# A batched matrix product: one batch per load with transposes on TensorE, against four batches per load with 32x32 transposes on VectorE

## Chip, cores and metric

One core of a Trainium2 chip runs the kernel. The metric is the device time of one execution in microseconds (us), taken as the median over several runs of the same program. The five engines of a core are called PE (TensorE; PEld is its loading of weights), DVE (VectorE), ACT (ScalarE), POOL (GpSimd) and SP (SyncE, which here only issues transfers). Sixteen DMA engines move data between the device memory (HBM) and the on-chip memory SBUF, which has 128 partitions. PE writes its results to a second on-chip memory, PSUM[...].

## What is computed

```python
# x: (32, 256, 512) float32, y: (32, 512, 384) float32
def reference(x, y):
    return np.einsum('bij,bjk->bik', x, y).astype(np.float32)
```

For each of 32 batches a 256 x 512 matrix is multiplied by a 512 x 384 matrix. The inputs are 41.94 MB, the output is 12.58 MB. PE sums over partitions, so the summed index j has to lie on the partitions of both operands. y arrives that way; x has to be transposed.

## The kernel before

Work is done one batch at a time. `load(b)` (L54 to L60) issues two transfers on SP's queue. Partition p of the x tile gets rows 2p and 2p+1 of the batch, 4 KB in one run; partition q of the y tile gets rows 4q to 4q+3, 6 KB in one run. So the j that lies on partition q in step t is 4q + t, for both operands.

`transpose(b)` (L62 to L72) makes x^T on PE: for each t of four it transposes the columns `t::NJ` of both row sets r with an identity matrix, in float32, into one PSUM tile (L68), which DVE (L70, t even) or ACT (L72, t odd) copies to SBUF as float16. `round_y(b)` (L74 to L81) rounds y to float16 in four pieces of 384 elements per partition, two on ACT (L79) and two on DVE (L81). `multiply(b)` (L83 to L99) does eight matmuls (L92), four steps t for each of two row sets r, each of which sums over 128 partitions and streams 384 columns. `collect(b)` copies the two results from PSUM to SBUF, one on ACT (L107) and one on DVE (L109), and `store(b)` (L120) issues one transfer of 3 KB per partition on SP.

What sets the order is the loop at L122 to L137 with `keep`, which keeps the instructions of each engine in program order. Five batches are loaded ahead. In step s the program loads batch s+5, collects s-2, transposes and rounds s, multiplies s-1 and stores s-2. In the last full step the matmuls come ahead of the transposes. All loads and stores share SP's queue, in this order, so a store that waits for its results holds back the loads written behind it. Buffers: seven each for x and y, eight for the output, four PSUM banks for transposes and four for results.

Of the kernel before, what the change touches and what calls it, by code (L numbers as in the profile page):

```python
# [1 line left out]

# [5 lines left out]


MM_DT = mybir.dt.float16  # L10
F32 = mybir.dt.float32
P = 128
AHEAD = 5
GROUPS = [1, 1, 1, 1, 1, 1, 1, 1, 1, 1, 1, 1, 1, 1, 1, 1, 1, 1, 1, 1, 1, 1, 1, 1, 1, 1, 1, 1, 1, 1, 1, 1]

@with_exitstack
def kernel(
    ctx: ExitStack,  # L20
    tc: tile.TileContext,
    x: bass.AP,
    y: bass.AP,
    out: bass.AP,
):
    nc = tc.nc

    B, I, J = x.shape
    _, _, K = y.shape

    NI = I // P
    NJ = J // P

    const_pool = ctx.enter_context(tc.tile_pool(name="const", bufs=1))
    x_pool = ctx.enter_context(tc.tile_pool(name="x_pool", bufs=AHEAD + 2))
    y_pool = ctx.enter_context(tc.tile_pool(name="y_pool", bufs=AHEAD + 2))
    yr_pool = ctx.enter_context(tc.tile_pool(name="yr_pool", bufs=4))
    xt_pool = ctx.enter_context(tc.tile_pool(name="xt_pool", bufs=4))
    o_pool = ctx.enter_context(tc.tile_pool(name="o_pool", bufs=8))
    tpsum_pool = ctx.enter_context(tc.tile_pool(name="tpsum", bufs=4, space=bass.MemoryType.PSUM))  # L40
    opsum_pool = ctx.enter_context(tc.tile_pool(name="opsum", bufs=4, space=bass.MemoryType.PSUM))


    keep = tc.keep_in_program_order

    identity = const_pool.tile([P, P], F32)
    make_identity(nc, identity)


    place = [(g, i, n) for g, n in enumerate(GROUPS) for i in range(n)]  # L50
    assert len(place) == B
    x_of, y_of, yr_of, xt_of, ps_of, o_of = {}, {}, {}, {}, {}, {}

    def load(b):  # L54


        x_of[b] = x_pool.tile([P, NI, J], F32, name="x_sb")
        y_of[b] = y_pool.tile([P, NJ, K], F32, name="y_sb")
        keep(nc.sync.dma_start(out=x_of[b], in_=x[b].rearrange("(p r) j -> p r j", p=P)))  # L59
        keep(nc.sync.dma_start(out=y_of[b], in_=y[b].rearrange("(q t) k -> q t k", q=P)))  # L60

    def transpose(b):  # L62
        x_sb = x_of.pop(b)
        xt_of[b] = xt_pool.tile([P, NJ, NI, P], MM_DT, name="xt_sb")
        for t in range(NJ):
            t_ps = tpsum_pool.tile([P, NI, P], F32, name="t_ps")
            for r in range(NI):
                keep(nc.tensor.transpose(t_ps[:, r], x_sb[:, r, t::NJ], identity))  # L68
            if t % 2 == 0:
                keep(nc.vector.tensor_copy(xt_of[b][:, t], t_ps))  # L70
            else:
                keep(nc.scalar.copy(xt_of[b][:, t], t_ps))  # L72

    def round_y(b):  # L74
        y_sb = y_of.pop(b)
        yr_of[b] = yr_pool.tile([P, NJ, K], MM_DT, name="y_r")
        for t in range(NJ):
            if t % 2 == 0:
                keep(nc.scalar.copy(yr_of[b][:, t], y_sb[:, t]))  # L79
            else:  # L80
                keep(nc.vector.tensor_copy(yr_of[b][:, t], y_sb[:, t]))  # L81

    def multiply(b):  # L83
        xt_sb, y_r = xt_of.pop(b), yr_of.pop(b)
        ps_of[b] = [
            opsum_pool.tile([P, K], F32, name=f"o_ps_{r}", tag="o_ps")
            for r in range(NI)
        ]
        for t in range(NJ):
            for r in range(NI):  # L90
                keep(
                    nc.tensor.matmul(  # L92
                        ps_of[b][r],
                        xt_sb[:, t, r],
                        y_r[:, t],
                        start=(t == 0),
                        stop=(t == NJ - 1),
                    )
                )  # L99

    def collect(b):
        g, i, n = place[b]
        if i == 0:
            o_of[g] = o_pool.tile([P, n, NI, K], F32, name="o_sb", tag=f"o_sb_{min(n, 2)}")
        for r in range(NI):
            if r % 2 == 0:
                keep(nc.scalar.copy(o_of[g][:, i, r], ps_of[b][r]))  # L107
            else:
                keep(nc.vector.tensor_copy(o_of[g][:, i, r], ps_of[b][r]))  # L109
        del ps_of[b]  # L110

    def store(b):
        g, i, n = place[b]
        if i < n - 1:
            return
        o_sb = o_of.pop(g)
        dst = out[b - i : b + 1].rearrange("b (p r) k -> p b (r k)", p=P)
        src = o_sb.rearrange("p b r k -> p b (r k)")
        if n == 1:
            keep(nc.sync.dma_start(out=dst[:, 0], in_=src[:, 0]))  # L120

    for b in range(AHEAD):  # L122
        load(b)
    for s in range(B + 2):
        if s + AHEAD < B:
            load(s + AHEAD)
        if s >= 2:
            collect(s - 2)
        if s == B - 1:
            multiply(s - 1)  # L130
        if s < B:
            transpose(s)
            round_y(s)
        if 1 <= s != B - 1 and s <= B:
            multiply(s - 1)
        if s >= 2:
            store(s - 2)  # L137


# [1 line left out]
_INS = ['x', 'y']  # L141
_OUTS = [((32, 256, 384), 'float32')]


# [23 lines left out]
```

## Time and profile before

| what | value |
|---|---|
| median of 8 runs | 137.29 us (137.19 to 137.57) |
| the profiled execution's own time | 137.42 us |
| its span, first to last instruction | 135.6 us |
| mean granted PE clock | 0.984 of full speed |
| busy: PE, PEld, DVE, ACT | 84.0, 58.6, 64.2, 66.7 us |
| DMA: bytes, mean rate | 54.64 MB, 403 GB/s |
| L68 transposes on PE, 256 | 40.6 us busy |
| L92 matmuls, 256 | 48.7 us busy, 336 ns mean of one |
| L70 and L72, transposes from PSUM, 64 each | 26.9 and 23.8 us busy, 423 and 372 ns |
| L79 and L81, rounding y, 64 each | 29.6 and 20.1 us busy, 509 and 355 ns |
| L109 and L107, results from PSUM, 32 each | 17.8 and 15.1 us busy, 557 and 471 ns |

The page cuts the span into 40 equal slices of 3.39 us. In the rows of engines each digit is the busy share of a slice in tenths; the DMA row is the mean share of the 16 DMA engines, and the row GB/s is what they moved. A row of a group names the line, the engine, the operation, the tile written and the tile read, the shape, how often it ran, its busy time and the mean duration of one. Consecutive instructions of an engine can overlap, so the busy time can be less than the count times the mean. The chain of waits goes back from the last instruction to what released it, and so on to the start; its shares say what the time was spent on.

### The profile page before, as it was taken

Reading aid. Unit: us, or ns where it says so; the run is one execution under the profiler, and the core shown is the slowest. Engines: PE = TensorE matmul, PEld = TensorE weight load, DVE = VectorE, ACT = ScalarE, POOL = GpSimd, SP = SyncE. Lnnn points to the kernel's source line nnn. Section 1 sums busy time; section 2 is a strip of 40 time slices with the busy share of each in tenths; the row PEclk is TensorE's granted clock in tenths of the full one; section 3 lists DMA queues with packets and bytes.
Section 4 is the critical chain, followed back from the end, with each engine's and each line's share of the span. In section 5 each row is a group of like instructions: output and inputs, shape, how many; then the busy total and the mean of one; then the engine's idle time right before and its main releaser. Section 6 shows DMA issues by size and latency. Waiting matters only on the chain.

```text
span 135.6 us, 1739 instructions
## 1 busy us (share of the span) xinstructions
PE 84.0 (62%) x512; PEld 58.6 (43%) x512; DVE 64.2 (47%) x160; ACT 66.7 (49%) x161; POOL 0.7 (1%) x6
## 2 busy tenths in 40 slices
PE   0579878855956765556765556775556775559610
PEld 0466555535534554334554333554333554335500
DVE  0344765643455544446544446544546544545510
ACT  3246866642556544456544456544456644446610
POOL 2000000000000000000000000000000000000000
PEclk9999999997799999999999999999999999999998
DMA  4999999999999999999999999999999999999992
GB/s 137 413 420 423 414 416 414 417 410 417 414 419 413 427 418 419 420 419 423 418 421 413 419 421 421 428 410 419 422 422 421 414 423 418 419 422 418 411 414 94
DMA packets 13833, 54.64 MB, mean 403 GB/s; under 512 B 1536, under 2 KB 1536, under 8 KB 13824
## 3 DMA queue, kind: packets, MB, share of 16 engines
q1 hardware_dynamic: 13824, 54.53, 98.6%
q8 instruction: 4, 0.07, 0.2%
q14 instruction: 5, 0.04, 0.1%
HBM read 41.94 MB, written 12.58 MB: 402 GB/s over the span
## 4 chain that ended last, share of the span: by engine, by line
DMA 90%; SPq 2%; PE 1%; issue 1%; DVE 0%; ACT 0%; ACTq 0%
DMA y_sb<-in_y_dram 43%; DMA out_dram<-o_sb 24%; DMA x_sb<-in_x_dram 23%; SPq L59 1%; PE o_ps L92 1%; SPq L60 1%; DVE o_sb L109 0%; ACT y_r L79 0%; SPq L120 0%; ACTq L79 0%
## 5 line engine op out<-in xcount | busy, mean ns | idle before, releaser
L68 PE MATMUL t_ps<-identity,x_sb 128*128 128x128 f32 x256 | 40.6, 305 | 44.1 <-DMA x_sb<-in_x_dram 41.5
L68 PEld LDWEIGHTS t_ps<-identity,x_sb 128*128 128x128 f32 x256 | 35.0, 211 | 54.8 <-DVE o_sb L109 44.0
L72 ACT CAST xt_sb<-t_ps 128x256 f16<-128x256 f32 x64 | 23.8, 372 | 52.5 <-issue 40.0
L92 PE MATMUL o_ps<-y_r,xt_sb 128*128 128x384 f16 x256 | 48.7, 336 | 1.2 <-ACT y_r L79 1.2
L70 DVE CAST xt_sb<-t_ps 128x256 f16<-128x256 f32 x64 | 26.9, 423 | 45.9 <-PE t_ps L68 44.0
L79 ACT CAST y_r<-y_sb 128x384 f16<-128x384 f32 x64 | 29.6, 509 | 7.4 <-DMA y_sb<-in_y_dram 7.3
L92 PEld LDWEIGHTS <-xt_sb 128*128 128x128 f16 x256 | 26.1, 102 | 15.6 <-issue 3.1
L81 DVE CAST y_r<-y_sb 128x384 f16<-128x384 f32 x64 | 20.1, 355 | 13.2 <-DMA y_sb<-in_y_dram 13.2
L109 DVE COPY o_sb<-o_ps 128x384 f32<-128x384 f32 x32 | 17.8, 557 | 6.6 <-PE o_ps L92 5.1
L107 ACT COPY o_sb<-o_ps 128x384 f32<-128x384 f32 x32 | 15.1, 471 | 2.4 <-PE o_ps L92 2.4
L72 ACT ACT_TABLE_LOAD x1 | 1.3, 1283 | 0.7 <-PEq L152 0.7
masks.py:199 POOL TENSOR_SCALAR_AFFINE_SELECT identity<-identity 128x128 f32<-128x128 f32 x1 | 0.3, 292 | 0.1
masks.py:197 POOL MEMSET identity<- 128x128 f32 x1 | 0.2, 205 | 0.3 <-POOLq L152 0.3
L152 POOL MEMSET const-bfloat16-1.0<- 128x1 bf16 x1 | 0.1, 101 | 0.0
L152 POOL MEMSET const-uint8-127<- 128x1 uint8 x1 | 0.1, 101 | 0.0
L152 POOL MEMSET const-float32-0.0<- 128x1 f32 x1 | 0.1, 98 | 0.2 <-issue 0.2
L152 POOL MEMSET const-float32-1.0<- 128x1 f32 x1 | 0.1, 98 | 0.0
## 6 DMA issues: line engine op xcount, KB each, us to landing
y_sb<-in_y_dram SPq DMA_DIRECT2D x32, 768.0 KB, 11.2
x_sb<-in_x_dram SPq DMA_DIRECT2D x32, 512.0 KB, 10.2
out_dram<-o_sb SPq DMA_DIRECT2D x32, 384.0 KB, 10.9
```

The source lines that it names most:

```text
L59: keep(nc.sync.dma_start(out=x_of[b], in_=x[b].rearrange("(p r) j -> p r j", p=P)))
L60: keep(nc.sync.dma_start(out=y_of[b], in_=y[b].rearrange("(q t) k -> q t k", q=P)))
L68: keep(nc.tensor.transpose(t_ps[:, r], x_sb[:, r, t::NJ], identity))
L70: keep(nc.vector.tensor_copy(xt_of[b][:, t], t_ps))
L72: keep(nc.scalar.copy(xt_of[b][:, t], t_ps))
L79: keep(nc.scalar.copy(yr_of[b][:, t], y_sb[:, t]))
L81: keep(nc.vector.tensor_copy(yr_of[b][:, t], y_sb[:, t]))
L92: nc.tensor.matmul(ps_of[b][r], xt_sb[:, t, r], y_r[:, t], start=(t == 0), stop=(t == NJ - 1),)
L107: keep(nc.scalar.copy(o_of[g][:, i, r], ps_of[b][r]))
L109: keep(nc.vector.tensor_copy(o_of[g][:, i, r], ps_of[b][r]))
L152: nc = _bacc.Bacc("TRN2", target_bir_lowering=False, num_devices=1)
```

## The change

Four batches form a chunk, and there are eight chunks. Each batch of a chunk has 32 of the 128 partitions.

- `load_x(n)` is one transfer of 2 MB: partition p of a batch's 32 gets rows 8p to 8p+7, 16 KB in one run. `load_y(n)` is one transfer of 3 MB: partition q gets rows 16q to 16q+15, 24 KB in one run. The last chunk's y comes in two transfers, 12 KB runs.
- `transpose_x(n)` no longer uses PE. ACT rounds x to float16 and lays out pairs of rows so that two float16 values make one 32-bit word, in four copies of 1024 elements per partition, reading with a step of 16 elements (64 bytes). After each, DVE transposes 32 x 32 blocks of such words, 512 words per partition. No identity matrix is made any more.
- `round_y(n)` rounds the chunk's y in eight pieces of 768 elements, five on DVE and three on ACT, in the order of `ROUND`.
- `multiply(n)` sums over 32 partitions at a time: for each of 16 steps c and two row sets e, four matmuls, one for each batch g, on that batch's 32 partitions, each into a PSUM bank of its own. That is 128 matmuls of 384 columns in a chunk, 1024 in all. All eight banks hold the results of one chunk.
- `collect(n)` is as before, eight copies for a chunk. `store(b)` still moves one batch, 3 KB per partition.
- The order: after the loads of x chunks 0 and 1 and y chunk 0, step n loads x chunk n+2 and y chunk n+1, rounds and multiplies chunk n, transposes chunk n+1, collects chunk n, and issues the stores of chunk n-1. The last two chunks' stores come last. There are two buffers each for x, the transposed x, y and rounded y, one for the packed x, and twelve for the output.

The diff, cut to its core:

```diff
--- before.py
+++ after.py
@@ -3,16 +3,22 @@
 import concourse.bass as bass
 import concourse.tile as tile
 from concourse import bass_utils, mybir
-from concourse.masks import make_identity
 from concourse._compat import with_exitstack
 MM_DT = mybir.dt.float16
 F32 = mybir.dt.float32
 P = 128
-AHEAD = 5
-GROUPS = [1, 1, 1, 1, 1, 1, 1, 1, 1, 1, 1, 1, 1, 1, 1, 1, 1, 1, 1, 1, 1, 1, 1, 1, 1, 1, 1, 1, 1, 1, 1, 1]
+Q = 4
+LATE = 8
+LAST = 2
+ROUND = (1, 0, 1, 1, 0, 1, 0, 1)
 @with_exitstack
@@ -28,113 +34,129 @@
     B, I, J = x.shape
     _, _, K = y.shape
-    NI = I // P
-    NJ = J // P
-    const_pool = ctx.enter_context(tc.tile_pool(name="const", bufs=1))
-    x_pool = ctx.enter_context(tc.tile_pool(name="x_pool", bufs=AHEAD + 2))
-    y_pool = ctx.enter_context(tc.tile_pool(name="y_pool", bufs=AHEAD + 2))
-    yr_pool = ctx.enter_context(tc.tile_pool(name="yr_pool", bufs=4))
-    xt_pool = ctx.enter_context(tc.tile_pool(name="xt_pool", bufs=4))
-    o_pool = ctx.enter_context(tc.tile_pool(name="o_pool", bufs=8))
-    tpsum_pool = ctx.enter_context(tc.tile_pool(name="tpsum", bufs=4, space=bass.MemoryType.PSUM))
-    opsum_pool = ctx.enter_context(tc.tile_pool(name="opsum", bufs=4, space=bass.MemoryType.PSUM))
+    S = P // Q
+    R = I // S
+    C = J // S
+    NE = I // P
+    A = R // NE // 2
+    N = B // Q
+    x_pool = ctx.enter_context(tc.tile_pool(name="x_pool", bufs=2))
+    xr_pool = ctx.enter_context(tc.tile_pool(name="xr_pool", bufs=1))
+    xt_pool = ctx.enter_context(tc.tile_pool(name="xt_pool", bufs=2))
+    y_pool = ctx.enter_context(tc.tile_pool(name="y_pool", bufs=2))
+    yr_pool = ctx.enter_context(tc.tile_pool(name="yr_pool", bufs=2))
+    o_pool = ctx.enter_context(tc.tile_pool(name="o_pool", bufs=12))
+    psum_pool = ctx.enter_context(tc.tile_pool(name="psum", bufs=Q * NE, space=bass.MemoryType.PSUM))
     keep = tc.keep_in_program_order
-    identity = const_pool.tile([P, P], F32)
-    make_identity(nc, identity)
+    x_of, y_of, xt_of, o_of = {}, {}, {}, {}
+    def load_x(n):
+        x_of[n] = x_pool.tile([P, R, J], F32, name="x_sb")
+        keep(
+            nc.sync.dma_start(
+                out=x_of[n],
+                in_=x[n * Q : (n + 1) * Q].rearrange("g (p r) j -> (g p) r j", r=R),
+            )
+        )
+    def load_y(n):
+        y_of[n] = y_pool.tile([P, C, K], F32, name="y_sb")
+        src = y[n * Q : (n + 1) * Q].rearrange("g (p c) k -> (g p) c k", c=C)
+        w = C // (LAST if n == N - 1 else 1)
+        for c in range(0, C, w):
+            keep(nc.sync.dma_start(out=y_of[n][:, c : c + w], in_=src[:, c : c + w]))
+    def transpose_x(n):
-    place = [(g, i, n) for g, n in enumerate(GROUPS) for i in range(n)]
-    assert len(place) == B
-    x_of, y_of, yr_of, xt_of, ps_of, o_of = {}, {}, {}, {}, {}, {}
-    def load(b):
-        x_of[b] = x_pool.tile([P, NI, J], F32, name="x_sb")
-        y_of[b] = y_pool.tile([P, NJ, K], F32, name="y_sb")
-        keep(nc.sync.dma_start(out=x_of[b], in_=x[b].rearrange("(p r) j -> p r j", p=P)))
-        keep(nc.sync.dma_start(out=y_of[b], in_=y[b].rearrange("(q t) k -> q t k", q=P)))
-    def transpose(b):
-        x_sb = x_of.pop(b)
-        xt_of[b] = xt_pool.tile([P, NJ, NI, P], MM_DT, name="xt_sb")
-        for t in range(NJ):
-            t_ps = tpsum_pool.tile([P, NI, P], F32, name="t_ps")
-            for r in range(NI):
-                keep(nc.tensor.transpose(t_ps[:, r], x_sb[:, r, t::NJ], identity))
-            if t % 2 == 0:
-                keep(nc.vector.tensor_copy(xt_of[b][:, t], t_ps))
-            else:
-                keep(nc.scalar.copy(xt_of[b][:, t], t_ps))
-    def round_y(b):
-        y_sb = y_of.pop(b)
-        yr_of[b] = yr_pool.tile([P, NJ, K], MM_DT, name="y_r")
-        for t in range(NJ):
-            if t % 2 == 0:
-                keep(nc.scalar.copy(yr_of[b][:, t], y_sb[:, t]))
-            else:
-                keep(nc.vector.tensor_copy(yr_of[b][:, t], y_sb[:, t]))
-    def multiply(b):
-        xt_sb, y_r = xt_of.pop(b), yr_of.pop(b)
-        ps_of[b] = [
-            opsum_pool.tile([P, K], F32, name=f"o_ps_{r}", tag="o_ps")
-            for r in range(NI)
-        ]
-        for t in range(NJ):
-            for r in range(NI):
+        x_sb = x_of.pop(n)
+        xr = xr_pool.tile([P, A, NE, C, S], F32, name="x_r")
+        xt = xt_pool.tile([P, C, NE, S, A], F32, name="xt_sb")
+        for a in range(A):
+            for e in range(NE):
                 keep(
-                    nc.tensor.matmul(
-                        ps_of[b][r],
-                        xt_sb[:, t, r],
-                        y_r[:, t],
-                        start=(t == 0),
-                        stop=(t == NJ - 1),
+                    nc.scalar.copy(
+                        xr[:, a, e].bitcast(MM_DT).rearrange("q c (j w) -> q w c j", w=2),
+                        x_sb[:, a * 2 * NE + e : (a + 1) * 2 * NE : NE].rearrange(
+                            "q w (j c) -> q w c j", c=C
+                        ),
                     )
                 )
+                keep(nc.vector.transpose(xt[:, :, e, :, a], xr[:, a, e]))
+        xt_of[n] = xt
-    def collect(b):
-        g, i, n = place[b]
-        if i == 0:
-            o_of[g] = o_pool.tile([P, n, NI, K], F32, name="o_sb", tag=f"o_sb_{min(n, 2)}")
-        for r in range(NI):
-            if r % 2 == 0:
-                keep(nc.scalar.copy(o_of[g][:, i, r], ps_of[b][r]))
+    def round_y(n):
+        y_sb = y_of.pop(n)
+        y_r = yr_pool.tile([P, C, K], MM_DT, name="y_r")
+        w = C // len(ROUND)
+        for k, dve in enumerate(ROUND):
+            part = slice(k * w, (k + 1) * w)
+            if dve:
+                keep(nc.vector.tensor_copy(y_r[:, part], y_sb[:, part]))
             else:
-                keep(nc.vector.tensor_copy(o_of[g][:, i, r], ps_of[b][r]))
-        del ps_of[b]
+                keep(nc.scalar.copy(y_r[:, part], y_sb[:, part]))
+        return y_r
+    def multiply(n, y_r):
+        xt_sb = xt_of.pop(n)
+        ps = [[psum_pool.tile([P, K], F32, name="o_ps") for e in range(NE)] for g in range(Q)]
+        for c in range(C):
+            for e in range(NE):
+                for g in range(Q):
+                    rows = slice(g * S, (g + 1) * S)
+                    keep(
+                        nc.tensor.matmul(
+                            ps[g][e],
+                            xt_sb[rows, c, e].rearrange("q p a -> q (p a)").bitcast(MM_DT),
+                            y_r[rows, c],
+                            start=(c == 0),
+                            stop=(c == C - 1),
+                        )
+                    )
+        return ps
+    def collect(n, ps):
+        for g in range(Q):
+            o_sb = o_of[n * Q + g] = o_pool.tile([P, NE, K], F32, name="o_sb")
+            for e in range(NE):
+                if e % 2 == 0:
+                    keep(nc.scalar.copy(o_sb[:, e], ps[g][e]))
+                else:
+                    keep(nc.vector.tensor_copy(o_sb[:, e], ps[g][e]))
     def store(b):
-        g, i, n = place[b]
-        if i < n - 1:
-            return
-        o_sb = o_of.pop(g)
-        dst = out[b - i : b + 1].rearrange("b (p r) k -> p b (r k)", p=P)
-        src = o_sb.rearrange("p b r k -> p b (r k)")
-        if n == 1:
-            keep(nc.sync.dma_start(out=dst[:, 0], in_=src[:, 0]))
+        keep(nc.sync.dma_start(out=out[b].rearrange("(m e) k -> m e k", m=P), in_=o_of.pop(b)))
-    for b in range(AHEAD):
-        load(b)
-    for s in range(B + 2):
-        if s + AHEAD < B:
-            load(s + AHEAD)
-        if s >= 2:
-            collect(s - 2)
-        if s == B - 1:
-            multiply(s - 1)
-        if s < B:
-            transpose(s)
-            round_y(s)
-        if 1 <= s != B - 1 and s <= B:
-            multiply(s - 1)
-        if s >= 2:
-            store(s - 2)
+    load_x(0)
+    load_x(1)
+    load_y(0)
+    transpose_x(0)
+    for n in range(N + 1):
+        if n + 2 < N:
+            load_x(n + 2)
+        if n + 1 < N:
+            load_y(n + 1)
+        if n < N:
+            ps = multiply(n, round_y(n))
+        if n + 1 < N:
+            transpose_x(n + 1)
+        if n < N:
+            collect(n, ps)
+        for b in range(max((n + 1) * Q - LATE, 0), min((n + 2) * Q - LATE, B) if n < N else B):
+            store(b)
 # ---- launch: one core; inputs and outputs as the reference has them ----
```

## The prediction

> **What bounds the kernel now.** I read the slices of the page first, then the DMA queues, the chain of waits, and last the windows and the groups.
>
> ```profile
> DMA  4999999999999999999999999999999999999992
> GB/s 137 413 420 423 414 416 414 417 410 417 414 419 413 427 418 419 420 419 423 418 421 413 419 421 421 428 410 419 422 422 421 414 423 418 419 422 418 411 414 94
> DMA packets 13833, 54.64 MB, mean 403 GB/s; under 512 B 1536, under 2 KB 1536, under 8 KB 13824
> q1 hardware_dynamic: 13824, 54.53, 98.6%
> DMA 90%; SPq 2%; PE 1%; issue 1%; DVE 0%; ACT 0%; ACTq 0%
> ```
>
> The 16 DMA engines are full from the second slice to the last but one; the chain is 90% transfers. No compute engine is above 62% of the span. So the time is bytes over rate, plus a start and an end. 13824 packets are 96 transfers of 128 runs (12288) and 1536 small ones, 16 for each transfer, which I take to be its completion. A run is now one packet: 4 KB for x, 6 KB for y, 3 KB for the output. The windows give the rate in steady state, at the end where only stores are left, and the clock around a pause of PE (columns: window and length; busy us and instructions of PE, PEld, DVE, ACT, POOL; clock; DMA share; GB/s):
>
> ```profile
> 40.00:60.00 20.00, 12.51 (x80) 8.72 (x80) 10.17 (x25) 10.23 (x25) 0.00 (x0) 1.00 1.02 420
> 130.00:130.50 0.50, 0.00 (x0) 0.00 (x0) 0.00 (x0) 0.00 (x0) 0.00 (x0) 1.00 1.01 406
> 130.50:131.00 0.50, 0.00 (x0) 0.00 (x0) 0.00 (x0) 0.00 (x0) 0.00 (x0) 1.00 1.03 418
> 30.00:32.00 2.00, 0.00 (x0) 0.02 (x1) 0.90 (x3) 1.08 (x3) 0.00 (x0) 1.00 0.98 405
> 32.00:34.00 2.00, 1.99 (x9) 1.83 (x10) 0.86 (x3) 0.39 (x2) 0.00 (x0) 0.54 1.05 430
> 34.00:36.00 2.00, 2.00 (x8) 0.83 (x6) 0.52 (x2) 1.20 (x4) 0.00 (x0) 0.61 1.00 408
> ```
>
> PE paused for 2.92 us and then ran about 3.5 us at a little over half its clock; the usual pauses of 1.6 to 2 us did not bring that. The timeline shows what it does to the eight matmuls of a batch:
>
> ```profile
> 33.74 2.36 PE L92 MATMUL o_ps<-y_r,xt_sb 128*128 128x384 f16 x8
> 41.52 1.46 PE L92 MATMUL o_ps<-y_r,xt_sb 128*128 128x384 f16 x8
> ```
>
> At full clock the last of eight lasts 0.326, so seven steps take 1.46 - 0.326 = 1.13 us, 162 ns each, and the weight loads between them are hidden. At half clock a step is twice that, 0.32.
>
> [...]
>
> **Part 1, the loads.** 64 loads become 8 of x (2 MB, 16 KB runs) and 9 of y (3 MB, 24 KB runs, the last in two halves); 32 stores stay as they are. Transfers fall from 96 to 49, runs from 12288 to 6272. The bytes, 54.53 MB, stay. At 420 GB/s they take 129.8 us[...]. A second reading: stores alone run at about 416 in 129 to 132 us, which takes 0.945 us for 0.393 MB; a batch at 420 takes 4.057 us, leaving 3.112 for its two loads of 1.311 MB. Solving for a cost per byte and per transfer gives 429 GB/s and 29 ns, so 47 x 29 ns = 1.4 us. That rests on half-microsecond readings from 406 to 424, so I take **2.2 us gained**. [...] Below nothing would need long runs that move slower than 4 KB ones; the trace cannot exclude it, and I keep 1 us for it.
>
> **Part 2, transposes and casts.** 256 transposes on PE (L68) and 128 copies from PSUM (L70, L72) go. In come 32 ACT copies of 1024 elements with x rounded[...] and 32 DVE transposes of 512 words. The trace has no DVE transpose: [...]it is about 0.69; twice that at worst. Rounding y is 24 ACT pieces of 768 (0.83 us) and 40 DVE pieces (355 ns plus 384 more at L81's pace, about 0.55). Collecting stays, 32 each at 471 and 557. A round of four batches costs ACT 3 x 0.83 + 4 x 1.04 + 4 x 0.47 = 8.5 us, DVE 5 x 0.55 + 4 x 0.69 + 4 x 0.56 = 7.8. Before it was 66.7/8 = 8.3 and 64.2/8 = 8.0. A round of transfers is 6.8 MB, 16 us. This is nothing while it lies under the transfers.
>
> **Part 3, the matmuls.** 1024 matmuls on 32 rows replace 256 on 128. If four run together, a pack of four takes 162 ns and a round 32 x 0.162 = 5.2 us. But PE now pauses about 9 us between rounds, so by the window above it starts at half clock: 3.5 us for 11 packs, then 21 x 0.162 = 3.4, with the last one's latency D = 7.1 us. In the middle that is hidden under 16 us.
>
> **Part 4, the start.** x0, x1 and y0 (7.34 MB) land at 2.3 (first bytes, from 182 GB/s in the first 4 us) + 17.1 + 0.8 (the first transposes started 0.8 us after their bytes were in) = 20.2 us. SP holds load 3 of x until ACT has rounded y0 (2.5) and copied x1 (4.2): 26.9. It must issue by 31.6 - 1.5 = 30.1 (1.5 us lie between the first issue and the first bytes). Slack 3.2 us, so nothing; copies at double cost just use it up. The loads of y wait only for rounding, done earlier; stores are eight batches late and wait for nothing on SP until the end.
>
> **Part 5, the end.** After y6 the queue holds four batches' stores, y7, then three times four batches' stores: 6.29 MB at 416 and 3.15 at 429, 22.4 us to the last byte. The four last stores need this chain after y6's bytes: landing 0.8, first rounding 0.5, D of round 6, four DVE collects 2.2 and rounding 0.55 (in program order on DVE ahead of the next matmuls), D of round 7, the first collect 0.56, issue to bytes 1.5, the stores 3.8: 9.9 + D6 + D7. There is room for D6 + D7 = 12.5. D6 is 7.1. D7 follows a pause of about 2.9 us, just where the trace had the clock fall: 5.4 if warm, 7.1 if not. The loss is 0 to 1.7; I take **0.9 lost**. y7's second half lands later than y6's chain needs only by less than this.
>
> **Sum.** The profiled execution took 137.42 (span 135.6 and 1.82 around it). -2.2 + 0.9 = -1.3 gives 136.1; it lies 0.13 above the median of the runs shown, so the forecast is **136.0**.
>
> **Rivals.** *The end of PE's chain takes the place of the queue* (slower): weight loads of 98 ns at full clock and 152 at half differ by 54 ns[...]; four in turn make a pack 213 ns, 427 at half clock. D is then 3.5 + 24 x 0.213 = 8.6, and the loss 2 x 8.6 - 12.5 = 4.7: 137.3 - 2.2 + 4.7 = 139.8. It decides once D6 + D7 passes 14.7. For it: a weight load for every 32-row matmul, four times as many. Against: the loads at L92 are hidden today, and different rows may load together. ACT reading x at a stride of 64 bytes[...] does the same: copies of 1.9 us hold DVE's collects of round 6 to about 10.7 us after landing, 3.1 late; 139.1. *Length of runs buys nothing*: rate 420 as today, end lost 0.9: 138.2. For it: loads and stores alone show nearly the same rate. *Row groups don't run together*, so the packing doesn't do what it says: 128 x 0.162 = 20.7 us plus 2.8 of collecting per round beats 16 us of transfers; 20.2 + 8 x 23.5 + about 10 = 218.
>
> **Chances.** Forecast with its neighbours 0.6 (its own range 133.9 to 137.4), long chain or strided copies 0.22, no gain from runs 0.14, no packing 0.04. A change below 0.2%, 0.27 us, is no change in what this kernel's measurement can tell: 0.1, taken from the upper end of the forecast and the lower end of the rivals. Faster 0.56, slower 0.34. The range leaves out no packing and the far ends: 133.5 to 140.3.
>
> **What would show it.** About 7056 packets; windows of 40 to 100 us at 427 GB/s rather than 420 (part 1); ACT copies of 1.04 us and DVE transposes of 0.69 (part 2); a round's matmuls in 7 us, with the clock low for their first half (part 3); no gap in the DMA slices before the last three (part 4); a dip below 1 us ahead of the last four stores (part 5). Wrong if the rate stays at 420, if the dip is over 2 us, or if the DMA row shows gaps in every round.

## The result

The changed kernel takes 141.17 us (median of 11 runs, 140.17 to 142.23), the kernel before 137.34 us (31 runs). The ratio is 1.0268, with a 95% interval of 1.0243 to 1.0293: 3.8 us slower, where 1.3 us faster was forecast, and above the top of the range (140.3). The profiled execution took 141.44, with a span of 139.7. From its page, in the order shown for the kernel before:

```profile
DMA  5999999999999999989999999999999999998056
GB/s 145 408 422 458 436 411 429 450 434 352 481 408 302 424 407 472 427 366 446 441 436 401 368 460 425 441 405 410 448 455 422 375 436 441 394 404 338 31 209 242
DMA packets 7068, 54.68 MB, mean 392 GB/s; under 512 B 785, under 2 KB 785, under 8 KB 4881
q1 hardware_dynamic: 7056, 54.53, 94.4%
DMA 65%; ACT 19%; PE 6%; issue 3%; DVE 2%; SPq 1%; DVEq 1%; ACTq 0%
```

The packets are halved (7056 against 13824 on the queue), as worked out. The DMA row is full until the last slices, and there it has a hole: 31 GB/s in slice 38, while the last stores wait to be made. ACT has come into the chain of waits with 19%. The row GB/s is more uneven than before, though its mean in the middle is hardly changed (418 GB/s below, 420 before). The windows of the changed kernel (columns as in the prediction) show the middle and the hole:

```profile
20.00:100.00 80.00, 39.66 (x688) 20.98 (x691) 38.04 (x70) 59.69 (x59) 0.00 (x0) 0.74 1.01 418
128.00:130.00 2.00, 2.00 (x32) 1.04 (x28) 0.00 (x0) 0.00 (x0) 0.00 (x0) 0.50 0.49 195
130.00:132.00 2.00, 2.00 (x52) 1.18 (x48) 0.00 (x0) 0.00 (x0) 0.00 (x0) 0.93 0.06 14
132.00:134.00 2.00, 0.86 (x24) 0.29 (x12) 1.11 (x3) 1.27 (x4) 0.00 (x0) 1.00 0.00 0
134.00:136.00 2.00, 0.00 (x0) 0.00 (x0) 0.84 (x2) 0.35 (x1) 0.00 (x0) 1.00 0.85 330
```

From about 129 to 134.3 us the DMA engines have next to nothing to do. The groups say which engine has grown dear:

```profile
L89 ACT CAST x_r<-x_sb 128x1024 f16<-128x1024 f32 x32 | 59.6, 1938 | 6.4 <-DMA x_sb<-in_x_dram 6.4
L96 DVE STREAM_TRANSPOSE xt_sb<-x_r 128x512 f32<-128x512 f32 x32 | 22.8, 713 | 49.2 <-ACT x_r L89 49.2
L108 ACT CAST y_r<-y_sb 128x768 f16<-128x768 f32 x24 | 18.4, 832 | 29.2 <-DMA y_sb<-in_y_dram 29.2
L106 DVE CAST y_r<-y_sb 128x768 f16<-128x768 f32 x40 | 19.5, 553 | 22.4 <-DMA y_sb<-in_y_dram 22.4
```

A regrouping copy on ACT takes 1.94 us instead of the 1.04 in the sum, the author's estimate, which the trace of before did not show. The other three durations, 0.71, 0.83 and 0.55 us, are those of the forecast (0.69, 0.83, 0.55) within 4%. The timeline of the last two chunks shows what the slow copies do (start, length, and in brackets the pause before it and its releaser):

```profile
112.06 2.30 ACT L108 CAST y_r<-y_sb 128x768 f16<-128x768 f32 x3 [4.74 <-DMA y_sb<-in_y_dram]
112.75 7.27 PE L120 MATMUL o_ps<-y_r,xt_sb 32*128 32x384 f16 x128 [9.21 <-DVE y_r L106]
113.05 0.15 PEld L120 LDWEIGHTS <-xt_sb 32*128 32x128 f16 x4 [0.16 <-issue]
113.37 0.15 PEld L120 LDWEIGHTS <-xt_sb 32*128 32x128 f16 x4 [0.17 <-issue]
114.27 7.44 ACT L89 CAST x_r<-x_sb 128x1024 f16<-128x1024 f32 x4
121.60 1.61 ACT L135 COPY o_sb<-o_ps 128x384 f32<-128x384 f32 x4
121.74 0.71 DVE L96 STREAM_TRANSPOSE xt_sb<-x_r 128x512 f32<-128x512 f32 x1 [1.12 <-ACT x_r L89]
122.37 1.91 DVE L137 COPY o_sb<-o_ps 128x384 f32<-128x384 f32 x4
124.81 8.05 PE L120 MATMUL o_ps<-y_r,xt_sb 32*128 32x384 f16 x128 [4.79 <-DVE y_r L106]
133.51 2.31 SPq L140 DMA_DIRECT2D out_dram<-o_sb  x4
```

Chunk 6 is multiplied by 112.75 + 7.27 = 120.02. DVE starts to collect it only at 122.37, 2.35 us later, because the transpose ahead of that on DVE waits for the last copy on ACT. So the next matmuls start late, after a pause of 4.79 us, run 8.05 us, and the last stores are issued at 133.51.

### The profile page after: what moved, and what is told of

Same layout as the page of the kernel before. It is cut to its first block, busy times and chain, and to the rows that moved or that the text cites. A ratio compares the mean times of both kernels' runs of the same rounds, so it can differ in the third digit from the quotient of the medians.

```text
span 139.7 us, 2433 instructions
## 1 busy us (share of the span) xinstructions
PE 58.5 (42%) x1024; PEld 30.8 (22%) x1024; DVE 57.0 (41%) x104; ACT 90.7 (65%) x89; POOL 0.2 (0%) x4
## 3 DMA queue, kind: packets, MB, share of 16 engines
q1 hardware_dynamic: 7056, 54.53, 94.4%
## 4 chain that ended last, share of the span: by engine, by line
DMA 65%; ACT 19%; PE 6%; issue 3%; DVE 2%; SPq 1%; DVEq 1%; ACTq 0%
DMA y_sb<-in_y_dram 42%; DMA out_dram<-o_sb 23%; ACT x_r L89 15%; PE o_ps L120 6%; ACT y_r L108 3%; DVE o_sb L137 1%; ACT o_sb L135 1%; DVE xt_sb L96 1%; SPq L65 1%; DVEq L185 0%; DVE y_r L106 0%; ACTq L135 0%; DVEq L137 0%; SPq L140 0%
## 5 line engine op out<-in xcount | busy, mean ns | idle before, releaser
L120 PE MATMUL o_ps<-y_r,xt_sb 32*128 32x384 f16 x1024 | 58.5, 398 | 74.3 <-DVE y_r L106 74.3
L89 ACT CAST x_r<-x_sb 128x1024 f16<-128x1024 f32 x32 | 59.6, 1938 | 6.4 <-DMA x_sb<-in_x_dram 6.4
L120 PEld LDWEIGHTS <-xt_sb 32*128 32x128 f16 x1024 | 30.8, 113 | 101.7 <-DVE y_r L106 55.8
L96 DVE STREAM_TRANSPOSE xt_sb<-x_r 128x512 f32<-128x512 f32 x32 | 22.8, 713 | 49.2 <-ACT x_r L89 49.2
L108 ACT CAST y_r<-y_sb 128x768 f16<-128x768 f32 x24 | 18.4, 832 | 29.2 <-DMA y_sb<-in_y_dram 29.2
L106 DVE CAST y_r<-y_sb 128x768 f16<-128x768 f32 x40 | 19.5, 553 | 22.4 <-DMA y_sb<-in_y_dram 22.4
L137 DVE COPY o_sb<-o_ps 128x384 f32<-128x384 f32 x32 | 15.3, 537 | 6.3 <-PE o_ps L120 6.3
L135 ACT COPY o_sb<-o_ps 128x384 f32<-128x384 f32 x32 | 12.9, 490 | 7.3 <-PE o_ps L120 7.3
```

What stands on the lines that cost most here:

```text
L89: nc.scalar.copy(xr[:, a, e].bitcast(MM_DT).rearrange("q c (j w) -> q w c j", w=2), x_sb[:, a * 2 * NE + e : (a + 1) * 2 * NE : NE].rearrange(
L96: keep(nc.vector.transpose(xt[:, :, e, :, a], xr[:, a, e]))
L106: keep(nc.vector.tensor_copy(y_r[:, part], y_sb[:, part]))
L108: keep(nc.scalar.copy(y_r[:, part], y_sb[:, part]))
L120: nc.tensor.matmul(ps[g][e], xt_sb[rows, c, e].rearrange("q p a -> q (p a)").bitcast(MM_DT), y_r[rows, c], start=(c == 0), stop=(c == C - 1),)
L135: keep(nc.scalar.copy(o_sb[:, e], ps[g][e]))
```

## The experiments

One theory and two rivals stood at the start. **Slow copies**: ACT's 1.94 us copies hold up the collecting at the end, and perhaps the first loads of x. **Rivals**: the end has too few stores behind it whatever the copies cost; or the long runs are themselves served worse. In the five kernels with no compute, or with plain copies, parts of the work are left out as the expectations say. The code below is cut to the lines that matter.

### Are the copies slow because of their strides?

The same four copies in their own order, so that reading and writing are contiguous:

```diff
-    xr[:, a, e].bitcast(MM_DT).rearrange("q c (j w) -> q w c j", w=2),
-    x_sb[:, a * 2 * NE + e : (a + 1) * 2 * NE : NE].rearrange("q w (j c) -> q w c j", c=C),
+    xr[:, a, e].bitcast(MM_DT).rearrange("q c (j w) -> q (c j w)", w=2).rearrange("q (w f) -> q w f", w=2),
+    x_sb[:, a * 2 * NE + e : (a + 1) * 2 * NE : NE],
```

> ACT copies x in its own order, reading and writing contiguously; the regrouping of columns and the pairing of rows are left out, so the product is of a shuffled x. Copies should take 1.04 us[...]. Theory of the slow copies: no late x loads, chunk 6 collected 1.9 us earlier, the second run of matmuls at the end 2 to 3 us earlier; 136 to 136.5. Rival, end too short of stores: about 139, with the dip of the DMA row at the end still over 4 us. Rival, uneven long runs: about 138.5.

Measured: 137.47 us, ratio to before 1.0005 (0.9986 to 1.0024). 3.7 us of the loss are gone. The row of the copy and the end of the timeline in this kernel:

```profile
L89 ACT CAST x_r<-x_sb 128x1024 f16<-128x1024 f32 x32 | 31.0, 1040 | 6.3 <-DMA x_sb<-in_x_dram 6.3
```
```profile
112.40 7.67 PE L118 MATMUL o_ps<-y_r,xt_sb 32*128 32x384 f16 x128 [8.83 <-DVE y_r L104]
120.10 1.95 DVE L135 COPY o_sb<-o_ps 128x384 f32<-128x384 f32 x4 [1.55 <-PE o_ps L118]
122.58 7.06 PE L118 MATMUL o_ps<-y_r,xt_sb 32*128 32x384 f16 x128 [2.51 <-DVE y_r L104]
```

A contiguous copy of 1024 elements takes 1.04 us, as the forecast's sum had it. DVE now waits for PE, not PE's results for DVE, and the second row of matmuls starts 2.2 us earlier. The time is 1 us above what was expected, so something else is left. This run takes away the read step of 64 bytes and the write step of 4 bytes together; it doesn't say which of them costs.

The same result in another order of elements, with the stride on the writing side:

```diff
-    ...rearrange("q c (j w) -> q w c j", w=2), ...rearrange("q w (j c) -> q w c j", c=C)
+    ...rearrange("q c (j w) -> q w j c", w=2), ...rearrange("q w (j c) -> q w j c", c=C)
```

> The same copy on ACT in another order of its elements: it reads x contiguously and writes with a step of 128 bytes, where it read with a step of 64 bytes and wrote with a step of 4. If it is the strided read that costs, copies fall from 1.94 to 1.04 us, and the time to about 136.5 (theory of the slow copies) or 139 (if the end has too few stores whatever the copies do). If strided writes cost as much, copies stay near 1.9 us and the time at 141.

Measured: 198.97 us, ratio 1.4486 (1.4451 to 1.4522); a copy takes 5.03 us.

```profile
L89 ACT CAST x_r<-x_sb 128x1024 f16<-128x1024 f32 x32 | 148.2, 5025 | 6.5 <-DMA x_sb<-in_x_dram 6.5
```

Neither case of the expectation: with contiguous reading and a write step of 128 bytes a copy takes 5.03 us, against 1.94 in the changed kernel, and the copies alone keep ACT busy for 148.2 of the span's 196.4 us. Then DVE first, reading x at the step of 64 bytes, and ACT rounding afterwards:

```diff
-    keep(nc.scalar.copy(xr[:, a, e]..., x_sb[...]...))
-    keep(nc.vector.transpose(xt[:, :, e, :, a], xr[:, a, e]))
+    for w in range(2):
+        row = a * 2 * NE + w * NE + e
+        keep(nc.vector.transpose(xr[:, a, e, w], x_sb[:, row].rearrange("q (j c) -> q c j", c=C)))
+    keep(nc.scalar.copy(xt[:, :, e, :, a].rearrange("q c s w -> q w c s"), xr[:, a, e]))
```

> DVE transposes 32x32 blocks of x in float32 straight from the loaded tile (eight instructions of 512 words, reading with the step of 64 bytes), and ACT then rounds 1024 elements contiguously, writing with a step of 8 bytes; the result is the same. If the strided read costs only ACT: DVE 0.71 us each as now, ACT 1.04, round loads DVE 10 us and ACT 8, and the time is near that of plain copies, 137.5. If DVE pays for the step as well, about double: 1.4 us each, 15.6 us a round on DVE, collecting late, and slower than the changed kernel, 145 or more.

Measured: 142.83 us, ratio 1.0416 (1.0379 to 1.0452).

```profile
L96 ACT CAST xt_sb<-x_r 128x1024 f16<-128x1024 f32 x32 | 75.1, 2540 | 19.8 <-DVE x_r L91 19.8
L91 DVE STREAM_TRANSPOSE x_r<-x_sb 128x512 f32<-128x512 f32 x64 | 60.8, 1015 | 8.3 <-DMA x_sb<-in_x_dram 8.3
```

The time lies between the two cases of the expectation. DVE pays for the step, but less than double: 1.02 us, against 0.71 in the changed kernel, where it reads contiguously and writes with a step of 8 bytes. The surprise is ACT: put at 1.04 us, its copy takes 2.54 when it writes float16 with a step of only 8 bytes, although it reads contiguously. The cost moved from one place to another. It also means that the write step of 4 bytes in the changed kernel may be what makes its copies 1.94 us. No run has the read step without a write step, or the write step of 4 bytes without the read step, so which of them costs is open.

### What do the transfers cost by themselves?

All compute left out; one constant tile is stored, and the loads and stores are issued in the order of each kernel. The cut for the changed kernel:

```diff
-    ps = multiply(n, round_y(n)); transpose_x(n + 1); collect(n, ps)
+    o_const = xr_pool.tile([P, NE, K], F32, name="o_c")      # stored by every store
```

> Transfers alone, as the kernel before issues them: 32 loads of x (4 KB runs), 32 of y (6 KB), 32 stores; all compute is left out and one constant tile is stored. The kernel before never starves its queue, so this should be its own time less the wait for the last results: about 136.5 us, 420 GB/s in the middle.

> Transfers alone, as the changed kernel issues them (8 loads of x in 16 KB runs, 9 of y in 24 KB runs, 32 stores, in its order); all compute is left out and one constant tile is stored. [...] 1.4 to 2.2 us less than the transfers of before. If it is per byte: the same. If long runs are served unevenly: more, 1 us or over.

> As the previous one, but every load is cut in four transfers of 4 KB runs (x) and 6 KB runs (y) with the same bytes in the same order; compute left out. Cost per transfer or packet: as the transfers of before. Only order and place matter: as the long runs.

The last of the three cuts each load:

```diff
+    for r in range(0, R, 2):
+        keep(nc.sync.dma_start(out=x_of[n][:, r : r + 2], in_=src[:, r : r + 2]))
...
+    w = C // 4
```

Measured: 136.60 us as before (ratio 0.9943, 0.9922 to 0.9964), 136.32 in the changed way (0.9932, 0.9907 to 0.9957), 139.73 in the changed way but in pieces (1.0190, 1.0139 to 1.0240). Windows of the kernel with the transfers of before and of the one with the changed transfers:

```profile
20.00:120.00 100.00, 0.00 (x0) 0.00 (x0) 1.00 1.02 418
```
```profile
20.00:120.00 100.00, 0.00 (x0) 0.00 (x0) 1.00 1.01 420
```

Here the columns after the length are DVE, POOL, clock, DMA share and GB/s. Half the transfers and half the packets are worth 0.3 us, and the intervals overlap. The eight runs of the changed transfers fall in two groups, 135.96 to 136.05 and 136.60 to 136.95 us, so against 136.60 a single run gains 0.6 us at most and can lose 0.3; the gain of 1.4 to 2.2 us, which a cost per transfer or per packet was expected to give, is in none of them. The third kernel fits neither case of its expectation, and it is no plain test of the length of runs: the transfers of before have as many 4 KB and 6 KB runs and need 136.60. What differs is that their 128 runs lie end to end in memory, while the pieces lie 16 KB and 24 KB apart, and that the transfers of before go one batch at a time through seven buffers each for x and y, the pieces one chunk at a time through two. Over the first 10 us the pieces moved 277 GB/s and the transfers of before 328, which is 1.2 of the 3.1 us. Which of the differences costs this was not tried further. The row GB/s of the changed transfers without any compute:

```profile
GB/s 116 422 442 459 386 422 461 437 451 398 463 429 386 359 420 398 420 424 384 432 412 432 404 418 430 454 437 382 433 442 442 437 362 454 421 401 417 414 384 66
```

It is nearly as uneven as in the changed kernel, with slices of 359 to 386 where no compute holds anything up. So most low slices of the changed kernel are not late loads of x. Its lowest before the end, 302 at about 42 to 45 us, has no equal here: from 44 to 48 us it moved 297 GB/s and these transfers 379, but in the next four 450 against 369. Over 20 to 100 us it moved 418 GB/s, these transfers 420.

The pieces in the whole kernel, for completeness:

> The changed kernel with every load of x and y cut in four transfers (4 KB and 6 KB runs as before), nothing else changed; the last y then comes in quarters instead of halves. If long runs gain 1.4 to 2.2 us where the queue is full, this is slower than the changed kernel by 1 to 2 us, about 142.5; if the length of runs buys nothing, the same, 141; if long runs are themselves served badly, faster.

Measured: 142.35 us, ratio 1.0384 (1.0362 to 1.0405) against 1.0268 for the changed kernel. That is the 1 to 2 us of the expectation, but after the run above it can't be read as the gain from long runs.

### Is the end short of stores, or held up?

```diff
-LATE = 8
+LATE = 12
-    o_pool = ctx.enter_context(tc.tile_pool(name="o_pool", bufs=12))
+    o_pool = ctx.enter_context(tc.tile_pool(name="o_pool", bufs=16))
```

> Stores are issued twelve batches late instead of eight (with sixteen output buffers), so that four more batches' stores, 3.7 us of transfers, stand behind the last load of y. Both theories of the end (slow copies or too few stores) expect its dip to shrink by about 3.7 us and the time to fall from 141.2 to about 137.5; the first rounds are the same. If the last loads do not land earlier for it, or the dip moves elsewhere, no change.

Measured: 139.09 us, ratio 1.0133 (1.0116 to 1.0150): 2.1 us of the 3.7. There is no trace of a typical execution, and where the other 1.6 us went is open. Both remedies together, the later stores and the plain copies:

> Contiguous ACT copies (the regrouping of x left out, as in the run with plain copies) and stores twelve batches late, both together. If slow copies and too few stores at the end are the two losses, neither is left: the time is that of the changed kernel's transfers alone plus about 1 us, and below the kernel before if long runs gain 1.4 to 2.2 us: 135 to 135.5. If long runs gain nothing, it ends at 137.

Measured: 136.98 us, ratio 0.9969 (0.9953 to 0.9985). The hole is closed, and the time is 0.7 us above the changed transfers alone. It beats the kernel before by 0.4 us and not by 1.4 to 2.2, which is the case of the expectation in which long runs gain nothing. Its windows:

```profile
126.00:128.00 2.00, 0.00 (x0) 0.00 (x0) 0.86 (x2) 0.37 (x1) 0.00 (x0) 1.00 1.02 406
128.00:130.00 2.00, 0.00 (x0) 0.00 (x0) 0.00 (x0) 0.00 (x0) 0.00 (x0) 0.69 0.98 392
```

### The same copies in another place

All four copies of the next chunk ahead of the rounding:

```diff
+        if n + 1 < N:
+            transpose_x(n + 1)
         if n < N:
             ps = multiply(n, round_y(n))
-        if n + 1 < N:
-            transpose_x(n + 1)
```

> One block moved: the transposes of chunk n+1 are put ahead of the rounding of chunk n, so ACT's four copies run while it would wait for y. Theory (slow copies in the way): in the changed kernel ACT's copies take 1.94 us each, and four of them lie between rounding and collecting; they delay the loads of x in the first rounds (a loss of some 2.5 us of transfers) and the collecting of chunk 6 by 1.9 us. Then the x loads are issued about 7 us earlier from load 3 on, chunk 6 is collected as soon as its matmuls end, and the time falls from 141.2 to about 136.5. Rival (long runs are served unevenly, the low slices of the DMA row come from the memory): the slices stay uneven and the time falls by at most the 2 to 3 us of the end, to about 138.5. Rival (end too short of stores): about 139.

Measured: 154.16 us, ratio 1.1157 (1.1101 to 1.1213), 13 us slower than the changed kernel. The expectation was plainly wrong, and a round of the timeline says why:

```profile
86.42 7.43 ACT L89 CAST x_r<-x_sb 128x1024 f16<-128x1024 f32 x4
93.72 2.33 ACT L108 CAST y_r<-y_sb 128x768 f16<-128x768 f32 x3
95.09 7.09 PE L120 MATMUL o_ps<-y_r,xt_sb 32*128 32x384 f16 x128 [10.03 <-DVE y_r L106]
102.05 1.63 ACT L135 COPY o_sb<-o_ps 128x384 f32<-128x384 f32 x4 [6.00 <-PE o_ps L120]
103.53 7.43 ACT L89 CAST x_r<-x_sb 128x1024 f16<-128x1024 f32 x4
```

Copies, rounding, matmuls and collecting now come one after the other, and ACT stands idle for 6 us under the matmuls. A round takes 103.53 - 86.42 = 17.1 us, more than the 16 of its transfers, so the loop bounds every round. In the changed kernel the copies lie under the matmuls; the harm seen at the end is the 2.35 us by which they outlast them. So half of them was moved, into the 4.7 us in which ACT waits for y:

```diff
+        if n + 1 < N:
+            transpose_x(n + 1, (0,))
         if n < N:
             ps = multiply(n, round_y(n))
         if n + 1 < N:
-            transpose_x(n + 1)
+            transpose_x(n + 1, (1,))
```

> The changed kernel with its result kept, but two of the four slow ACT copies of chunk n+1 (and their DVE transposes) are put ahead of the rounding of chunk n, in the 4.7 us in which ACT waits for y, and two stay behind. If the copies cost only what they hold up (the collecting of chunk 6, by 1.9 us, and through a longer pause of PE another 1 us), this is as good as contiguous copies: 137.5. If it is their length as such, or the order matters otherwise (all four ahead made it 154), the time stays at 141 or above.

Measured: 136.93 us, ratio to before 0.9987 (0.9971 to 1.0004); 4.2 us less than the changed kernel and 0.6 below the expectation, with copies as slow as they were (3.76 to 3.78 us for two in a row, where four took 7.44). Its timeline at the end:

```profile
111.50 2.44 DVE L107 CAST y_r<-y_sb 128x768 f16<-128x768 f32 x5 [1.92 <-DMA y_sb<-in_y_dram]
112.12 8.07 PE L121 MATMUL o_ps<-y_r,xt_sb 32*128 32x384 f16 x128 [8.42 <-DVE y_r L107]
120.22 1.95 DVE L138 COPY o_sb<-o_ps 128x384 f32<-128x384 f32 x4 [2.00 <-PE o_ps L121]
122.69 5.38 PE L121 MATMUL o_ps<-y_r,xt_sb 32*128 32x384 f16 x128 [2.51 <-DVE y_r L107]
128.72 2.31 SPq L141 DMA_DIRECT2D out_dram<-o_sb  x4
```

Collecting follows the matmuls at once. From the landing of y6 (111.50) to the first of the last stores it is 17.2 us; in the changed kernel it was 133.51 - 112.06 = 21.5. Part of this is luck of the profiled execution: the second run of matmuls took 5.38 us, and 7.06 after the same pause in the run with plain copies. The move also lets loads 3 and 4 of x go out 3.5 and 3.3 us earlier (26.75 and 40.36), but y6 landed only 0.56 us earlier for it. With later stores added:

> As the previous run, with stores twelve batches late (sixteen output buffers). If the end is then covered by stores, the time is that of the run with contiguous copies and late stores, 137.0, just below the kernel before; the transfers alone, 136.3, are the floor. If the first x loads still come late, so that no store fills the queue there, it stays near 138 to 139.

Measured: 137.07 us, ratio 0.9975 (0.9961 to 0.9990). No better than half the copies alone, and both are level with the kernel before or 0.3% ahead of it, 0.6 to 0.8 us above the transfers alone. Only one of the two closes the hole: from 128 to 130 us the DMA engines are busy for 0.44 of the time with half the copies moved alone, and for 0.98 with the later stores too. With the later stores the last bytes trail instead, at shares of 0.80 and 0.11 in the next two windows of 2 us, against 1.01 and 0.77. So the kernel with this hole is no slower than the one without it; why is open.

## Why the prediction was wrong

The sum was -2.2 + 0.9. In the same terms, with the transfers alone as the measure of the first: 136.32 - 136.60 = -0.3. What compute adds to its own transfers was 0.8 in the kernel before (137.42 in that comparison, against 136.60) and is 4.85 in the changed one (141.17 - 136.32), which is +4.0. Together about +3.8, the measured 141.17 - 137.34. So two terms failed: the gain of part 1, put at 2.2 us, was about 0.3, and the loss of part 5, put at 0.9 us, was about 4.0, most of it through the price of ACT's copies in part 2.

**Part 1 failed**: it counted on a cost per transfer or per packet. Its 2.2 us were the author's estimate, from a rate above 420 GB/s that the kernel before showed over no 20 us. Half the packets save 0.3 us, and from 40 to 100 us, where the forecast wanted 427 GB/s, the changed kernel moved 418, its transfers alone 415, and the kernels with plain copies and with half the copies moved 420 and 421. The solution that gave 29 ns per transfer rested on half-microsecond readings, as the text said; loads with stores and stores alone showed nearly the same rate (420 GB/s from 40 to 60 us, 416 from 129 to 132), which was the evidence to follow. The named rival, that the length of runs buys nothing, held to within the 0.6 us that single runs of the transfers alone still allow.

**Part 2** mis-sized one term: 4 x 1.04 us of ACT copies measured 4 x 1.94 less their overlap, 7.4 us in a row. That this could be so was in the text as a rival, with copies of 1.9 us, the author's estimate; the forecast took the low end though the trace had no strided read to set against it. That 1.94 was measured doesn't show that the reading costs it, since the write step of 4 bytes was there too. With contiguous reading and a write step of 8 bytes the copy took 2.54 us, and with one of 128 bytes 5.03. The 0.69 us of a DVE transpose, measured as 0.71, is what L70 and L109 give when their times for 256 and 384 elements (423 and 557 ns) are carried on to 512. ACT's round is then 90.7/8 = 11.3 us, not 8.5; that still lies under 16.

**Part 3 held**: here four matmuls on different sets of 32 rows ran at the pace of one. Packs start 0.32 us apart at half clock, as the weight loads above show (granted clock 0.50 from 112.75 to 116 us), and D is 6.7 to 8.05 us over the eight rounds, 7.0 to 7.3 in four of them, against 7.1. Those rows also settle the first rival: four weight loads together take 0.15 us, and one of the kernel before took a mean of 147 ns from 32.5 to 35 us (granted clock 0.54 to 0.61), so they aren't queued behind each other.

**Part 4** had the mechanism right and the time wrong, mostly by the same copies: load 3 of x was issued 3.4 us later than the 26.9 of the forecast, and 0.2 past the limit of 30.1.

```profile
30.29 0.33 SPq L65 DMA_DIRECT2D x_sb<-in_x_dram  x1
```

Little is lost by it: the rate over 20 to 100 us is 418 against 420 for the transfers alone, and y6 landed at 112.06, 0.56 us later than with half the copies moved. My later belief that the first rounds had lost 2.5 us fell with that.

**Part 5**: the chain is the one described; two terms were too small. From y6 to the last stores the forecast had 3.8 + D6 + D7 = 17.2 with its D6 + D7 = 13.4. Measured it is 0.69 to the first matmul, D6 = 7.27, 2.35 of waiting for the copies, 1.91 and 0.53 for collecting and rounding, D7 = 8.05, 0.65 to the issue: 21.45. So 2.35 us were the copies, named as a rival (3.1), and 1.9 us D6 + D7 = 15.3. The copies made the pause ahead of the second run 4.79 us, not 2.9, and after pauses over 4 us the 128 matmuls took 6.70 to 8.05 us in the eight rounds of the changed kernel and 6.90 to 8.19 in later rounds of the experiments, against 5.38 at full clock (granted 1.00 from 122 to 128 us, half the copies moved). Within that span D doesn't grow with the pause (6.97 after 4.20 us, with stores twelve batches late; 8.05 after 4.79; 7.09 after 10.03, with all copies ahead), so what made this D7 8.05 and not 7.1 is open. The experiment that moved half of the copies brought the chain back to 17.2 us and the time down by 4.2 us. That it is the 17.2 of the forecast is in part luck: D6 was 8.07 there, not 7.1, and D7 5.38.

The rival with strided copies was put at 139.1, with the full gain from long runs in it; with no such gain it would have been near 141. Two of the named cases came true together, and the range didn't add them. That this comes so close is luck too: the wait was 2.35 us and not 3.1, and D6 + D7 was longer.

## What to carry to other kernels

Here the queue of transfers was full, and half as many, longer transfers changed 0.3 us of 137. Before counting on such a gain, run the transfers alone, with compute left out, a few times. Most of the rest was decided at the end of the program: list the steps between the last load that counts and the last store, with each in-order engine's other work in between, and see whether the queued stores cover them. Work that is long but hidden could stay long here; it had to be placed where its engine waited anyway, without letting it stand in line with the rest.

## What the hardware showed

- ACT's copy of 1024 float32 elements to float16 differed with its steps: 1.04 us contiguous (the run with plain copies), 1.94 reading at 64 bytes and writing at 4 (the changed kernel), 2.54 writing at 8 (DVE first) and 5.03 writing at 128 (strided writing), both read contiguously. Whether the 1.94 comes from its reading or its writing is not shown. DVE's 32x32 transpose of 512 words took 0.71 us when it read contiguously and wrote at 8 bytes (the changed kernel), and 1.02 when it read at 64 bytes and wrote contiguously (DVE first).
- Four matmuls on 32 rows with four weight loads of their own went at the pace of one on 128 rows, for packs in a row: 0.32 us at half clock (the changed kernel, granted clock 0.50 from 112.75 to 116 us), and 5.38 us for 32 packs at full clock (half the copies moved, granted 1.00 from 122 to 128 us), that is, 0.17 each, against 0.162 for one matmul on 128 rows in the kernel before (seven steps of the 1.46 us for eight).
- After a pause of PE of 2.51 us the next 128 matmuls took 5.38 us in one execution (half the copies moved, granted clock 1.00 from 122 to 128 us) and 7.06 in three others: with plain copies (0.50 from 124 to 126 us), with these and later stores, and with half the copies moved and later stores (0.50 from 119 to 121 us).
- With compute left out, loads in 128 runs of 4 or 6 KB that lie end to end moved about as fast as loads in runs of 16 and 24 KB (418 and 420 GB/s from 20 to 120 us; 136.60 and 136.32 us in all). Loads in runs of 4 and 6 KB at a pitch of 16 and 24 KB took 139.73 us (414 GB/s from 20 to 120 us); that the pitch is the cause is not shown.
